# Rounding plain weight blocks by transfers: casting and adding DMAs in place of an ACT cast and a DVE subtract

## The chip, the cores and the metric

The kernel runs on one core of a Trainium2 chip. The metric is the device time of one execution in microseconds (us), lower is better. The core has five engines with their own instruction streams: TensorE (PE, matmuls; PEld are its weight loads), VectorE (DVE), ScalarE (ACT), GpSimd (POOL) and SyncE (SP), beside 16 DMA engines that the streams of SP, ACT and POOL can feed. The engines meet through semaphores only; each runs its own stream in order.

## The reference

One inference step of a decoder layer on 560 token columns: 16 meta tokens, 512 prompt tokens, 32 new tokens of 8 running sequences. With D = 1024 and a feed-forward width of 2816 = 22 x 128:

```python
x = x + 0.5 * swiglu(rmsnorm(x, g1), w_gate1, w_up1, w_down1)     # FFN1
x = x + mixer(rmsnorm(x, gm), ...)                                # mLSTM heads and RG-LRU
x = x + 0.5 * swiglu(rmsnorm(x, g2), w_gate2, w_up2, w_down2)     # FFN2
y = rmsnorm(x, gf)
```

where `swiglu(x, g, u, d) = (silu(x @ g) * (x @ u)) @ d`. Everything is fp32. The change touches the two FFNs only.

## The kernel before

**Three products for one.** PE multiplies in fp32r, a rounded fp32. To keep fp32's precision each operand is split into a rounded part `hi` and its remainder `lo`, and a product becomes three: hi by hi, hi by lo, lo by hi (`split_mm`, the matmuls are L295). Weights come from HBM in units of 128 x 512 (the down projections' in part 128 x 384). Of each unit the first product reads `whi`, the second `whi` again, the third `wlo`, for each of its 128-column pieces, so PE needs `wlo` about 0.5 us behind the unit's first matmul.

**The weight pipeline.** `units` lists all weight units in the order of use, each with a kind. Kind `""` is a plain block. The kinds "11", "s2", "s1" and so on belong to the seven-product form, in which the later blocks of both FFNs are multiplied from sums of quarters. For a plain unit there are three steps before: `load` puts an SP transfer into a `raw` tile, `split_hi` rounds it on ACT (a cast, L258) into `whi`, `split_lo` subtracts on DVE (L263) into `wlo`. Each fetch of a unit (`next_w`) first calls `run_ahead`, which emits the load of the unit 8 ahead, sums 6 ahead, the cast 5 ahead and the subtract 4 ahead (`AHEAD = 8, 6, 5, 4`). `raw`, `whi` and `wlo` have six buffers each, so a unit's tile is free when the unit six before it has been multiplied.

**Plain blocks at the beginnings.** A block is 128 of the 2816 hidden columns: a gate product g, an up product u (two units each) and a part of the down products d0 to d7. FFN1 has the first 4 blocks plain (`PLAIN = 4, 3`), FFN2 the first 3. FFN1 starts with pieces of block 0, loaded by code of its own; then come g1, u1, g2, u2, g3, u3 and the down units d4, d0, d2, d6, d5, d3, d1, d7. FFN2 has g0, u0, g1, u1, g2, u2 and eight down units of 384 columns. Everything behind is in the seven-product form.

**What sets the order.** PE, ACT and DVE are in `MANUAL`: their instructions stay in the order in which the program emits them, and that order is written out in the lists `FF1`, `FF2`, `MID1` and `MID2` as step names. POOL and SP are ordered by a scheduler. Of the steps, `g2` or `u1` are products, `eg`/`eu` scale them into `z`, `sg` is the Silu on ACT (L538), `mu`, `hh` and `hl` make the hidden tile and its two parts (L534, L544, L547); `ya`/`yb` form the normalised input `xn` for the seven-product form (DVE, L553), `Ah`, `Bh`, `Eh` and `Fh` round pieces of it on ACT (L560, tiles q11h, q21h, qt1h, qt4h), `ta` to `td` make its differences on DVE (L574 to L586). These steps are spread between the plain products. The piece of FF1 that matters here:

```python
... hh0 Ah1 u1 sg1 Bh1 hl0 Al1 eu1 g2 mu1 u2 ta1 Bl1 tb1 hh1 eg2 eu2 ...
```

A product step emits the ACT and DVE work of `run_ahead` at its own place in their streams, so a cast or subtract stands among the steps that are listed there. POOL does little in the FFNs: it adds up squares for the norms (`acc`, L377).

Of the kernel before, what the change touches and what calls it, by code (L numbers as in the profile page):

```python
# [5 lines left out]
F32 = mybir.dt.float32  # L6
F32R = mybir.dt.float32r
AF = mybir.ActivationFunctionType
ALU = mybir.AluOpType
PSUM = bass.MemoryType.PSUM  # L10

P = 128
# [4 lines left out]
TQ = T - C16  # L17
NP = 528
Q = 280
AHEAD = 8, 6, 5, 4  # L20
MANUAL = {mybir.EngineType.PE, mybir.EngineType.Activation, mybir.EngineType.DVE}
TCUT = 304
DED = 7
# [115 lines left out]
def hymba_step(ctx, tc, xT, wgu1, wdn1, win, wout, wgu2, wdn2, consts, small, c0t, wrg,  # L139
               y, o_small, o_m, o_cp, o_cs):  # L140
    nc = tc.nc
    act, dve, pool, pe = nc.scalar, nc.vector, nc.gpsimd, nc.tensor
# [10 lines left out]

    units = []

    def plain_units(w, n=1024):
        units.extend(("", w[:, c:min(c + 512, n)]) for c in range(0, n, 512))

    def units7(quarters):
        old = None  # L160
        for q in quarters:
            units.append(("11", q))
            if old is not None:
                units.extend((k, old) for k in ("22", "s4"))
            units.extend((k, q) for k in (("s2", "s1", "s3", "12") if old is not None else ("12", "s2", "s1", "s3")))
            old = q
        units.extend((k, old) for k in ("22", "s4"))

    def down_units(wdn, d, a, b):
        for i in range(a, b, 4):  # L170
            plain_units(wdn[d, :, i * P:min(i + 4, b) * P], (min(i + 4, b) - i) * P)

    def blocks(ff):


        a, b = PLAIN[ff], PLAIN[ff] + 8
        return (0, a), (a, b), {"d": (b, KF), "e": (b, FT), "t": (FT, KF)}

    def ff_units(ff, wgu, wdn, plan, mid):
        plain, seven, rest = blocks(ff)  # L180
        for t in plan:
            if t[0] in "gu" and t[1:].isdigit() or t[:2] == "ga":
                plain_units(wgu[int(t.lstrip("gua")), "gu".index(t[0])])
            elif t[0] == "d" and t[1:].isdigit():
                down_units(wdn, int(t[1:]), *plain)
        units7({"11": w[0, :, :512], "12": w[0, :, 512:], "21": w[1, :, :512], "22": w[1, :, 512:]}
               for w in (wgu[f] for f in range(seven[0], KF)))
        q = {}
        for t in mid:
            what, d = t[:-1], t[-1]  # L190
            if what in rest:
                down_units(wdn, int(d), *rest[what])
            elif what == "qa":
                lo, hi = (slice(i * P, i * P + 512) for i in (seven[0], seven[0] + 4))
                u, v = wdn[int(d)], wdn[int(d) + 4]
                q[d] = {"11": u[:, lo], "12": u[:, hi], "21": v[:, lo], "22": v[:, hi]}
            if what[:1] == "q":
                units.append((SEVEN[what[1]][0], q[d]))
    ff_units(0, wgu1, wdn1, FF1, MID1)
    for i in range(25):  # L200
        plain_units(win[i])
    for d in range(KD):
        plain_units(wout[d])
    ff_units(1, wgu2, wdn2, FF2, MID2)
    for d in range(TAIL, KD):
        down_units(wdn2, d, FT, KF)
    loaded, ready = {}, {}
    state = {"use": 0}

    def raw_tile():  # L210
        return wp.tile([P, 512], F32, tag="raw", name="raw")

    def hl_tile():
        return (wp.tile([P, 512], F32R, tag="hi", name="whi"), wp.tile([P, 512], F32R, tag="lo", name="wlo"))
# [6 lines left out]
    def load(i):  # L221
        kind, src = units[i]
        if not kind:
            loaded[i] = raw_tile()
            nc.sync.dma_start(loaded[i][:, :src.shape[-1]], src)
        for k in {"11": ("11",), "s2": ("21", "22"), "12": ("12",)}.get(kind, ()):
            t = raw_tile()
            nc.sync.dma_start(t, src[k])
            src[k] = t

    def quarter_sum(q, k):

        if k in q:
            return
        q[k] = q["s2"] if k == "s4" else sp.tile([P, 512], F32, tag="s", name=k, bufs=4)
        x, y, op = {"s1": ("21", "22", ALU.add), "s2": ("s1", "11", ALU.subtract),
                    "s3": ("11", "21", ALU.subtract), "s4": ("12", "s2", ALU.subtract)}[k]
        dve.tensor_tensor(q[k], q[x], q[y], op=op)  # L238

    def sums(i):  # L240
        kind, q = units[i]
        for k in {"s2": ("s1", "s2"), "s3": ("s3",)}.get(kind, ()):
            quarter_sum(q, k)
        b = units[i - 1 - AHEAD[1] + AHEAD[3]]
        if b[0] == "s2":
# [5 lines left out]
    def source(i):  # L251
        kind, q = units[i]
        return q[kind] if kind else loaded[i][:, :q.shape[-1]]

    def split_hi(i):
        ready[i] = hl_tile()
        src = source(i)
        act.copy(ready[i][0][:, :src.shape[-1]], src)  # L258

    def split_lo(i):  # L260
        src = source(i)
        hi, lo = (t[:, :src.shape[-1]] for t in ready[i])
        dve.tensor_tensor(lo, src, hi, op=ALU.subtract)  # L263

    def run_ahead(i):
        for fn, n in zip((load, sums, split_hi, split_lo), AHEAD):
            for j in range(state.get(fn, 0), min(i + n, len(units) - 1) + 1):
                fn(j)
                state[fn] = j + 1

    def up_to(i):
        for fn, n in ((load, 4), (sums, 0), (split_hi, 0), (split_lo, 0)):
            for j in range(state.get(fn, 0), i + n + 1):
                fn(j)
                state[fn] = j + 1

    def next_w(ahead=True):
        i = state["use"]
        state["use"] += 1
        if ahead:  # L280
            run_ahead(i)
        return ready.pop(i)
# [65 lines left out]
    class Norm:  # L348
# [38 lines left out]
        def mean(self):  # L387
            self.ps = [aux_tile("psn")[:, :(T - self.c0) // 2] for _ in range(2)]
            for hf in range(2):
                pe.matmul(self.ps[hf], one_m[1024], self.acc[:, self.half(hf)], start=True, stop=True)  # L390
            self.t = tmp("rn")
# [114 lines left out]
    def ffn(ff, nrm, c0, hp, plan, mid, steps):  # L506
# [87 lines left out]
        def rd(what):  # L594
            def fn(d):
                resid(ps[what, d], d, c0)
            return fn

        steps.update(ga=first_half, gb=second_half, g=product("g"), u=product("u"), pn=nrm.mean, rs=nrm.table, nw=nrm.step, eg=scaled("g"), eu=scaled("u"), sg=sg, mu=mu,
                     hh=hh, hl=hl, ya=y(0), yb=y(1), ta=ta, tb=tb, tc=tc_, td=td, d=dn("d", *plain), rd=rd("d"), v=run_ahead)  # L600
        for name, i, names, w in (("A", 0, ("11",), n), ("B", 1, ("21", "22"), 2 * n), ("E", 0, ("t1", "t3"), 2 * n),
                                  ("F", 1, ("t4", "t2"), 2 * n)):
# [117 lines left out]
    with tc.tile_pool(name="hp2", bufs=1) as hp, tc.tile_pool(name="sp2", bufs=1) as sp:  # L720
# [26 lines left out]
        w = [[next_w() for i in range(2)] for d in range(TAIL, KD)]  # L747
# [33 lines left out]
        with tc.manual_schedule(engines=MANUAL):  # L781
# [3 lines left out]
            a, b = parts[0]  # L785
            last_mm(1, TAIL, fs[:4])
            ps, t = mean(0)
# [11 lines left out]
            a, b = parts[1]  # L799
            ps, t = mean(1)  # L800
# [791 lines left out]
```

## Time and profile before

| | us |
|---|---|
| median of 3 runs | 1029.77 (1029.45 to 1031.06) |
| the profiled execution, its own time | 1030.47 |
| span of its profile | 1028.7 |
| mean granted clock of PE | 0.997 |

The profile is of one execution. Engine busy times are on its page; chains of waits name what released each step; a window's row gives busy time by engine, the granted TensorE clock and what the DMA engines moved. In a timeline row an entry such as `x3 1.89` is three instructions in a row that take 1.89 us together, and `[1.61 <-DVE xn L553]` is idle time ahead of it and what ended that. The plain blocks of FFN1 lie between 15 and 85 us, those of FFN2 between 651 and 708 us.

### The profile page before, as it was taken

To read this page: it belongs to the slowest core of one execution; us is meant where nothing else is said; L and a number is where in the kernel's file an instruction comes from. 1 tells how busy PE (TensorE), PEld (TensorE's weight loads), DVE (VectorE), ACT (ScalarE), POOL (GpSimd) and SP (SyncE) were. 2 spreads that over 40 slices of the span, in tenths; PEclk is the share of its full clock that TensorE was granted. 3 is DMA by queue.
4 is the path that set the end of the run, shared out by engine and by line. 5 is a ranking of instruction groups with operands and counts; after the bars stand their busy time and mean duration, and the time that the engine had idled before them with its cause. 6 is when DMAs were issued, how large, how long until landed. Compare 5 with 4: busy or idle time off the path is not lost.

```text
span 1028.7 us, 20136 instructions
## 1 busy us (share of the span) xinstructions
PE 1009.9 (98%) x7786; PEld 994.2 (97%) x7786; DVE 835.1 (81%) x1453; ACT 558.0 (54%) x1071; POOL 114.3 (11%) x178
## 2 busy tenths in 40 slices
PE   9999999999999999999999999999999999999996
PEld 8999999999999999989889999999999999999996
DVE  7988788888778797888878775789888889859774
ACT  6544555565544455575856643554555566653543
POOL 0000000000000043544442101100000000000003
PEclk9999999999999999999999999999999999999999
DMA  6322323233332334224132123123332323333222
GB/s 217 104 82 87 99 93 113 84 102 103 88 103 68 105 102 138 92 64 128 62 107 86 62 92 120 59 68 101 103 104 93 113 93 103 95 109 93 72 76 87
DMA packets 57543, 99.57 MB, mean 97 GB/s; under 512 B 7904, under 2 KB 14688, under 8 KB 57448
## 3 DMA queue, kind: packets, MB, share of 16 engines
q1 hardware_dynamic: 57304, 98.17, 30.3%
q8 instruction: 61, 1.00, 0.4%
q14 instruction: 34, 0.28, 0.1%
q10 hardware_dynamic: 144, 0.12, 0.0%
HBM read 93.57 MB, written 4.70 MB: 96 GB/s over the span
## 4 chain that ended last, share of the span: by engine, by line
PE 86%; DVE 6%; ACT 3%; issue 2%; POOL 1%; DMA 1%; SPq 0%; DVEq 0%; ACTq 0%; POOLq 0%
PE pb L408 27%; PE pad L408 20%; PE pd L295 14%; PE po L295 6%; PE pg L295 3%; PE pu L295 3%; PE py L295 2%; DVE wlo L263 1%; PE pv L295 1%; PE pk L295 1%; PE pq L295 1%; PE pd L762 1%; PE pn L1370 1%; PE p L295 1%; PE px L295 1%
## 5 line engine op out<-in xcount | busy, mean ns | idle before, releaser
L258 ACT CAST whi<-raw 128x512 fp32r<-128x512 f32 (+2 forms) x289 | 172.6, 606 | 164.6 <-PE pad L408 41.9
L263 DVE TENSOR_TENSOR wlo<-raw,whi 128x512 fp32r<-128x512 f32 (+2 forms) x289 | 197.1, 698 | 69.0 <-ACT whi L258 68.8
L258 ACT CAST whi<-s 128x512 fp32r<-128x512 f32 x180 | 111.8, 621 | 106.1 <-PE pb L408 36.5
L263 DVE TENSOR_TENSOR wlo<-s,whi 128x512 fp32r<-128x512 f32 x180 | 124.2, 691 | 12.7 <-ACT whi L258 6.5
L408 PE MATMUL pad<-q21h,whi 128*128 128x280 f32 (+1 forms) x360 | 104.2, 289 | 0.9 <-ACT whi L258 0.9
L408 PE MATMUL pb<-qt4l,whi 128*128 128x280 f32 (+1 forms) x360 | 104.0, 289 | 0.0
L408 PE MATMUL pad<-q21l,whi 128*128 128x280 f32 (+1 forms) x360 | 104.0, 289 | 0.0
L408 PE MATMUL pad<-q21h,wlo 128*128 128x280 f32 (+1 forms) x360 | 104.0, 289 | 0.0
L408 PE MATMUL pb<-qt4h,whi 128*128 128x280 f32 (+1 forms) x360 | 103.9, 289 | 0.0
L408 PE MATMUL pb<-qt4h,wlo 128*128 128x280 f32 (+1 forms) x360 | 103.9, 289 | 0.0
L408 PEld LDWEIGHTS pad<-q21h,whi 128*128 128x128 f32 x360 | 67.8, 188 | 1.1 <-ACT whi L258 1.1
L408 PEld LDWEIGHTS pb<-qt4h,whi 128*128 128x128 f32 x360 | 67.9, 189 | 0.0
L408 PEld LDWEIGHTS pb<-qt4h,wlo 128*128 128x128 f32 x360 | 67.8, 188 | 0.0
L408 PEld LDWEIGHTS pad<-q21l,whi 128*128 128x128 f32 x360 | 67.8, 188 | 0.0
L408 PEld LDWEIGHTS pb<-qt4l,whi 128*128 128x128 f32 x360 | 67.8, 188 | 0.0
L408 PEld LDWEIGHTS pad<-q21h,wlo 128*128 128x128 f32 x360 | 67.8, 188 | 0.0
L377 POOL TENSOR_TENSOR acc<-acc,sq 128x560 f32<-128x560 f32 (+1 forms) x12 | 18.1, 1512 | 442.9 <-ACT sq L376 442.7
L238 DVE TENSOR_TENSOR s<-raw 128x512 f32<-128x512 f32 x90 | 61.5, 683 | 2.1 <-DMA raw<-in_wdn 2.1
L295 PE MATMUL pd<-hl,whi 128*128 128x280 f32 (+1 forms) x294 | 61.6, 291 | 0.8 <-DVE hl L547 0.8
L295 PE MATMUL pd<-hh,whi 128*128 128x280 f32 (+1 forms) x294 | 61.3, 290 | 0.8 <-ACT hh L544 0.8
L295 PE MATMUL pd<-hh,wlo 128*128 128x280 f32 (+1 forms) x294 | 61.2, 289 | 0.0
L408 PE MATMUL pb<-q11h,whi 128*128 128x280 f32 (+1 forms) x180 | 52.4, 291 | 0.0
(456 smaller groups left out, 2978.6 us busy)
## 6 DMA issues: line engine op xcount, KB each, us to landing
raw<-in_wgu SPq DMA_DIRECT2D x174, 256.0 KB, 2.9
raw<-in_wdn SPq DMA_DIRECT2D x71, 256.0 KB, 2.8
raw<-in_win SPq DMA_DIRECT2D x50, 256.0 KB, 2.9
raw<-in_wout SPq DMA_DIRECT2D x16, 256.0 KB, 2.7
raw<-in_wdn SPq DMA_DIRECT2D x18, 192.0 KB, 2.4
c<-in_c0t SPq DMA_DIRECT2D x4, 512.0 KB, 3.5
out_o_cs<-c SPq DMA_DIRECT2D x4, 512.0 KB, 4.5
X<-in_xT SPq DMA_DIRECT2D x7, 280.0 KB, 4.3
```

Source lines behind the costliest of these rows:

```text
L238: dve.tensor_tensor(q[k], q[x], q[y], op=op)
L258: act.copy(ready[i][0][:, :src.shape[-1]], src)
L263: dve.tensor_tensor(lo, src, hi, op=ALU.subtract)
L295: state["mm"] = pe.matmul(ps[:, hf, :n], a[:, ws], b[k][:, c0 + hf * n:c0 + hf * n + n], start=first and j == 0 and i == 0, stop=last and ...
L377: (dve if d == KD - 1 else pool).tensor_tensor(self.acc[:, c0:], self.acc[:, c0:], s[:, c0:], op=ALU.add)
L408: pe.matmul(ps, a[:, k * P:k * P + P], b, start=first and k == 0 and i == 0, stop=k == KD // 2 - 1 and i == 2, skip_group_check=not first)
L762: pe.matmul(pd[d - TAIL][:, hf, :b - a], u[:, o:o + P], v[:, C16 + a:C16 + b], start=f == c0 and m == 0, stop=f == c1 - 1 and m == 2)
L1370: pe.matmul(pn[:, 0, a:512], V[:KROWS[i], i, :P], W[:KROWS[i], WO[i]:WO[i] + 512 - a], start=i == 0, stop=i == 4)
```

## The change

Units of plain blocks behind the first four of the program get the kind "dma": g2, u2, g3, u3 and the eight down units of FFN1 (16 units), and all plain units of FFN2 (20). For these,

- `load` puts out no SP transfer, and no `raw` tile is used;
- `split_hi` is a transfer from HBM on POOL's queue whose destination is fp32r, so that the transfer rounds (L264);
- `split_lo` does nothing;
- a fifth stage, `rest`, 3 units ahead, writes the negative of `whi` into `wlo` on ACT (L273), and a second transfer on POOL's queue adds the same weights from HBM to it (L274): `wlo = -whi + w`.

Per unit this is one SP transfer, one ACT cast and one DVE subtract less, and one ACT negative and two POOL transfers more. Lines behind the change move by 18 (the matmuls of L295 are L313, q11h's cast of L560 is L578).

```diff
-AHEAD = 8, 6, 5, 4
+AHEAD = 8, 6, 5, 4, 3
...
         for t in plan:
+            kind = "dma" if ff or len(units) > 3 else ""
...
-                plain_units(wgu[int(t.lstrip("gua")), "gu".index(t[0])])
+                plain_units(wgu[int(t.lstrip("gua")), "gu".index(t[0])], kind=kind)
...
-                down_units(wdn, int(t[1:]), *plain)
+                down_units(wdn, int(t[1:]), *plain, kind)
...
     def load(i):
...
+        if kind == "dma":
+            return
...
     def split_hi(i):
         ready[i] = hl_tile()
+        kind, src = units[i]
+        if kind == "dma":
+            pool.dma_start(ready[i][0][:, :src.shape[-1]], src)
+            return
         src = source(i)
         act.copy(ready[i][0][:, :src.shape[-1]], src)
 
+    def rest(i):
+        kind, src = units[i]
+        if kind == "dma":
+            hi, lo = (t[:, :src.shape[-1]] for t in ready[i])
+            act.mul(lo, hi.bitcast(F32), -1.0)
+            pool.dma_start(lo, src, accum_op=ALU.add)
+
     def split_lo(i):
+        if units[i][0] == "dma":
+            return
...
     def run_ahead(i):
-        for fn, n in zip((load, sums, split_hi, split_lo), AHEAD):
+        for fn, n in zip((load, sums, split_hi, split_lo, rest), AHEAD):
```

ACT's stream in FFN1, from the cast of u1's second half on (whi_403 before, whi_391 now). Before, 406 and 409 are the two halves of g2, 412 and 468 those of u2, 498 the first of g3:

```order
L258 CAST whi_403<-raw_315 128x512
L258 CAST whi_406<-raw_317 128x512
L258 CAST whi_409<-raw_328 128x512
L258 CAST whi_412<-raw_376 128x512
L560 CAST qt1h0_444<-xn_383 128x560
L560 CAST qt4h0_452<-xn_385 128x560
L544 CAST hh0_129<-z_394 128x560
L560 CAST q11h1_462<-xn_457 128x280
L258 CAST whi_468<-raw_397 128x512
L258 CAST whi_498<-raw_399 128x512
```

The same stretch now, where 394/395 and 397/398 are the rounded part and rest of g2's halves, and 400/401 of u2's first:

```order
L267 CAST whi_391<-raw_315 128x512
L273 ACTIVATE wlo_395<-whi_394 128x512
L578 CAST qt1h0_432<-xn_377 128x560
L578 CAST qt4h0_440<-xn_379 128x560
L562 CAST hh0_129<-z_388 128x560
L578 CAST q11h1_450<-xn_445 128x280
L273 ACTIVATE wlo_398<-whi_397 128x512
L273 ACTIVATE wlo_401<-whi_400 128x512
L556 ACTIVATE z_438<-z_438 128x560
```

Both halves of g2 were rounded on ACT ahead of qt1h0; now the negative of the second half stands behind q11h1, and its adding transfer behind that.

POOL's stream in FFN1 behind the constants, now (before, nothing stood there up to FFN1's end; 483 and 521 are g3's halves, 455 the second of u2):

```order
L264 DMA whi_483<-in_wgu1 128x512
L274 DMA wlo_395<-in_wgu1 128x512
L264 DMA whi_521<-in_wgu1 128x512
L274 DMA wlo_398<-in_wgu1 128x512
L274 DMA wlo_401<-in_wgu1 128x512
L274 DMA wlo_455<-in_wgu1 128x512
L274 DMA wlo_484<-in_wgu1 128x512
```

Casting transfers, which wait for a free buffer, and adding ones, which wait for ACT's negative, alternate in one queue at first.

ACT's stream in FFN2's down units, before:

```order
L560 CAST qt4h2_8791<-xn_8767 128x544
L258 CAST whi_8797<-raw_8664 128x384
L560 CAST q11h3_8822<-xn_8819 128x272
```

and now, where 8668 is the rest of the fourth down unit and 8697 of the fifth:

```order
L578 CAST qt4h2_8749<-xn_8725 128x544
L273 ACTIVATE wlo_8668<-whi_8667 128x384
L578 CAST q11h3_8781<-xn_8778 128x272
L273 ACTIVATE wlo_8697<-whi_8696 128x384
L273 ACTIVATE wlo_8756<-whi_8755 128x384
```

The cast that stood there was of a later unit (the sixth); now it is the fourth unit's negative, with a transfer still to come.

POOL's stream at the beginning of FFN2, now; before, the three acc rows stood there without a transfer between them:

```order
L264 DMA whi_8124<-in_wgu2 128x512
L274 DMA wlo_8096<-in_wgu2 128x512
L395 TENSOR_TENSOR acc_5034<-acc_5034,sq_8185 128x544
L264 DMA whi_8151<-in_wgu2 128x512
L274 DMA wlo_8125<-in_wgu2 128x512
L264 DMA whi_8189<-in_wgu2 128x512
L274 DMA wlo_8152<-in_wgu2 128x512
L395 TENSOR_TENSOR acc_5034<-acc_5034,sq_8252 128x544
```

The accumulations of FFN2's norm now stand behind the transfers of its first units.

More of the change, by code (lines that the diff above doesn't have):

```diff
@@ L154, in hymba_step, with plain_units @@
     units = []
-    def plain_units(w, n=1024):
-        units.extend(("", w[:, c:min(c + 512, n)]) for c in range(0, n, 512))
+    def plain_units(w, n=1024, kind=""):
+        units.extend((kind, w[:, c:min(c + 512, n)]) for c in range(0, n, 512))
     def units7(quarters):
@@ L167, in units7, with down_units @@
         units.extend((k, old) for k in ("22", "s4"))
-    def down_units(wdn, d, a, b):
+    def down_units(wdn, d, a, b, kind=""):
         for i in range(a, b, 4):
-            plain_units(wdn[d, :, i * P:min(i + 4, b) * P], (min(i + 4, b) - i) * P)
+            plain_units(wdn[d, :, i * P:min(i + 4, b) * P], (min(i + 4, b) - i) * P, kind)
     def blocks(ff):
```

## The prediction

> **What bounds the kernel now.** I read the page first: the busy line, then the chain of waits by engine, then the transfer rates of the first slices.
>
> ```profile
> span 1028.7 us, 20136 instructions
> PE 1009.9 (98%) x7786; PEld 994.2 (97%) x7786; DVE 835.1 (81%) x1453; ACT 558.0 (54%) x1071; POOL 114.3 (11%) x178
> GB/s 217 104 82 87 99 93 113 84 102 103 88 103 68 105 102 138 92 64 128 62 107 86 62 92 120 59 68 101 103 104 93 113 93 103 95 109 93 72 76 87
> PE 86%; DVE 6%; ACT 3%; issue 2%; POOL 1%; DMA 1%; SPq 0%; DVEq 0%; ACTq 0%; POOLq 0%
> ```
>
> TensorE is busy for 98% of the span and holds 86% of the chain. So work taken from DVE or ACT buys nothing in itself; it counts where PE waits. How much waiting there is, the windows over the plain blocks show: three over FFN1's (15 to 85 us), two over FFN2's (651 to 708 us). Columns are the window, its length, the busy time (instructions) of PE, PEld, DVE, ACT and POOL, the granted clock, the DMA share and GB/s.
>
> ```profile
> 15.00:35.00 20.00, 19.04 (x139) 18.18 (x138) 17.31 (x31) 10.57 (x18) 0.00 (x0) 1.00 0.33 108
> 35.00:62.00 27.00, 27.00 (x210) 26.83 (x208) 22.45 (x37) 12.94 (x24) 0.00 (x0) 1.00 0.34 108
> 62.00:85.00 23.00, 22.75 (x175) 22.47 (x175) 21.96 (x38) 8.67 (x16) 0.00 (x0) 1.00 0.24 81
> 651.00:690.00 39.00, 38.70 (x306) 38.32 (x304) 32.34 (x58) 20.58 (x38) 1.67 (x2) 1.00 0.21 65
> 690.00:708.00 18.00, 16.99 (x132) 16.77 (x133) 17.93 (x33) 7.66 (x14) 0.00 (x0) 1.00 0.31 102
> ```
>
> PE's idle time there is 0.96 + 0 + 0.25 + 0.30 + 1.01 = 2.5 us. That is all that this change could win, and all that now covers it is lead time: how long before PE reads a weight half the half is ready.
>
> **What falls away.** 36 units (16 in FFN1, 20 in FFN2; 28 of 512 columns, 8 of 384) lose their SP load, ACT cast and DVE subtract.
>
> ```profile
> L258 ACT CAST whi<-raw 128x512 fp32r<-128x512 f32 (+2 forms) x289 | 172.6, 606 | 164.6 <-PE pad L408 41.9
> L263 DVE TENSOR_TENSOR wlo<-raw,whi 128x512 fp32r<-128x512 f32 (+2 forms) x289 | 197.1, 698 | 69.0 <-ACT whi L258 68.8
> L377 POOL TENSOR_TENSOR acc<-acc,sq 128x560 f32<-128x560 f32 (+1 forms) x12 | 18.1, 1512 | 442.9 <-ACT sq L376 442.7
> raw<-in_wgu SPq DMA_DIRECT2D x174, 256.0 KB, 2.9
> raw<-in_wdn SPq DMA_DIRECT2D x18, 192.0 KB, 2.4
> c<-in_c0t SPq DMA_DIRECT2D x4, 512.0 KB, 3.5
> Eb<-rows SPq DMA_DIRECT2D x4, 272.0 KB, 4.7
> ```
>
> DVE loses about 36 x 0.698 = 25 us of busy time (a little less for the 384-wide), all beside PE: 0 us on the path. ACT exchanges a cast of 0.606 for a negative of the same shape, one for one: 0 on the path as long as ACT stays near half busy (10.57 of 20.00 in the first window). The weights are read twice, 28 x 256 KB + 8 x 192 KB = 9 MB more; FFN1's 4.2 MB over 70 us are 60 GB/s beside 81 to 108, and the page's first slice moved 217, so bandwidth costs 0. If that cover were gone, it would lengthen each landing, which the upper bound below holds.
>
> **What is added: a longer tail behind each rounded half.** Before, the second half of a weight block was one DVE instruction of 0.698 us behind the cast. Now it is a negative on ACT, an issue on POOL's queue, and a transfer from HBM that adds into the tile. I call T the time from the start of that issue to the landing, and I the time of one POOL issue. The trace has neither a POOL transfer nor an adding one. T's lower bound is the fastest SP row of this size, 2.4 us (192 KB); the upper is the slowest, 4.7 (272 KB), and 0.6 for a slower issue: 5.3. I is bounded by SP's issue below (0.43) and a POOL TENSOR_TENSOR above (1.512).
>
> ```profile
> 5.06 0.43 SPq L633 DMA_DIRECT2D raw<-in_wgu  x1
> ```
>
> I take I = 1.0, the middle. I take T = 3.8: a transfer that also reads its destination moves between once and twice its bytes, so 2.9 (256 KB) to 3.5 (512 KB), and I - 0.43 = 0.6 more to issue gives 3.5 to 4.1. One page has a price: the Trainium skill, "DMA: Bandwidth & Descriptors", section "Anatomy of one DMA — SWDGE (gpsimd) path", fits 2.0 us + bytes/436e3 per transfer from this queue, an estimate of 2.6 us for 256 KB and a sum lower by 1.2; no run here shows it yet.
>
> **FFN1: the place that sets the end.** The new stage is emitted only 3 units ahead, and ACT's order puts the negative of g2's second half (wlo_398) behind q11h1, a step of Ah1 that waits for DVE's xn. The timeline of before at that place:
>
> ```profile
> 31.31 1.89 DVE L263 TENSOR_TENSOR wlo<-raw,whi 128x512 fp32r<-128x512 f32 x3
> ...
> 37.87 1.51 DVE L553 SCALAR_TENSOR_TENSOR xn<-X,C,r 128x560 f32<-128x560 f32 x2
> ...
> 38.37 0.42 PE L295 MATMUL pg<-xh,wlo 128*128 128x280 f32 x2
> ...
> 38.70 0.43 ACT L560 CAST q11h<-xn 128x280 fp32r<-128x280 f32 x1 [1.61 <-DVE xn L553]
> ...
> 39.03 0.62 ACT L258 CAST whi<-raw 128x512 fp32r<-128x512 f32 x1
> ```
>
> PE first reads that half at 38.37. Of the three subtracts at 31.31, two (g2's) are gone: 2 x 0.63 = 1.26 us. If DVE is earlier by all of it, q11h1 starts at 38.70 - 1.26 = 37.44 and ends at 37.87; the negative, 0.62 like the cast at 39.03, ends at 38.49; with 0.07 for a signal (38.70 less the first xn's end, 37.87 + 0.755) POOL issues at 38.56. The half lands at 38.56 + T, so PE is late by T + 0.2 = **4.0 us** (2.6 and 5.5 at T's bounds). If DVE's waits, 2.7 us in the first window, eat the 1.26, it is T + 1.45. On POOL only the casting transfer of g3 stands between; it waits for a buffer that u1's last matmul frees at 34.90 (chain row below) and is issued by 36. The earlier half of g2 may stall PE too; that moves PE's clock of needs, not the landing at 42.4, so the two don't add. The units behind follow one issue (1.0) apart while PE takes 6.21 / 2 = 3.1 us for each: covered. Queued on ACT behind the negative are u2's negative and g1's Silu; neither waits for POOL.
>
> ```profile
> 34.90 6.21 PE pg L295 x48
> ...
> 574.88 7.55 PE py L295 x48
> ...
> 588.96 6.03 PE py L295 x48
> ...
> 651.15 6.01 PE pg L295 x48
> ...
> 691.52 16.68 PE pd L295 x130
> ```
>
> **FFN2.** The tightest place is the fourth down unit (wlo_8668), whose negative stands behind qt4h2:
>
> ```profile
> 692.49 0.65 ACT L560 CAST qt4h<-xn 128x544 fp32r<-128x544 f32 x1 [2.09 <-DVE xn L586]
> 693.04 0.51 ACT L258 CAST whi<-raw 128x384 fp32r<-128x384 f32 x1
> ...
> 697.18 0.42 PE L295 MATMUL pd<-hh,wlo 128*128 128x272 f32 x2
> ```
>
> Negative to 693.04 + 0.51 = 693.55, issue at 693.6, landing at 693.6 + T against a need at 697.18: late by T - 3.6 = **0.2 us** (0 and 1.7 at the bounds).
>
> **The clock.** Chains show one unit pair on PE taking 7.55 us where the same work later took 6.03. The windows around the first, and around the 1.0 us of idle at 690:
>
> ```profile
> 569.00:574.00 5.00, 5.00 (x29) 3.54 (x28) 3.16 (x7) 4.34 (x8) 1.59 (x1) 1.00 0.02 3
> 574.00:578.00 4.00, 4.00 (x20) 3.96 (x21) 2.89 (x5) 2.97 (x7) 0.32 (x1) 0.57 0.00 0
> 690.00:693.00 3.00, 1.99 (x13) 1.77 (x14) 2.97 (x7) 0.91 (x2) 0.00 (x0) 1.00 0.00 0
> ```
>
> After 5 us of thin matmul work the granted clock fell to 0.57 and cost 7.55 - 6.03 = 1.5 us; after 1.0 us of idle it stayed at 1.00. A stall of 4 us with nothing at all is nearer the first: **+1.5 us**, between 0 and 1.5. The Trainium skill, "TensorE: Matmul & The Clock Gate", section "What's actually happening", says that a free-running window of about 3.4 us without activity halves the clock; a 4.0 us stall need not hold a whole window, so by that rule the term could be 0. The trace's fall after thin, not empty, work speaks for more.
>
> **Sum.** Against the profiled execution: 1030.47 + 4.0 + 0.2 + 1.5 = 1036.2 us. That execution lies 0.7 above the median of the runs, so the median comes to **1035.5 us**, +0.56%. Bounds: 1029.77 + 2.6 = 1032.4 (T = 2.4, no clock) to 1029.77 + 6.75 + 1.7 + 1.5 = 1039.7.
>
> **Rivals.**
>
> *B, POOL becomes the bound.* FFN2 has 40 issues. The first can't go before a hi buffer is free, five units of 6.01 / 2 = 3.0 us ahead of 651.15: 636.1. The last down unit starts about 2.3 us before the chain's end at 708.2 and reads its second half 0.5 later; less T, its issue must start by 702.6. In those 66.5 us POOL also does three accumulations for the norm:
>
> ```profile
> 653.26 1.37 POOL L377 TENSOR_TENSOR acc<-acc,sq 128x544 f32<-128x544 f32 x1 [1.96 <-ACT sq L376]
> ```
>
> (66.5 - 4.1) / 39 = 1.60 us for each issue: from I = 1.6 POOL decides. At I = 1.75 FFN2 pays 39 x 0.15 = 5.9, FFN1 T = 4.55 and so 4.75, the clock 1.5: 1029.77 + 12.1 = 1041.9. For it: in-order waits on negatives cost POOL some of that time, and those accumulations, which gate FFN2's norm, now queue behind transfers. Against: 1.6 is above the 1.51 of a whole elementwise pass on this engine. The Trainium skill, "SBUF — State Buffer", section "A bandwidth-pool intuition that's wrong (but worth ruling out)", has such a transfer grow from 620 to 3100 ns beside a DVE copy that shuts POOL out; its section "Who interferes with whom" infers that two-input subtracts, the rows here, leave descriptor writing alone. By the first, an issue that waits for one DVE instruction of 0.698 is an estimate of I = 1.7, in B.
>
> *C, hidden.* T below 1.9 us, or a DVE so much earlier that the negative no longer stands behind q11h1's wait: within 2.06 us of before, about 1029.8. Against: no SP row of 192 KB or more lands under 2.4, and DVE would have to gain 4 us there, not 1.26.
>
> *D, faster.* DVE's waits for casts and the late hh/hl at 690 to 693 close because 36 subtracts are gone, and PE's 2.5 us of idle with them: 1029.77 - 2.5 = 1027.3. It decides only if the negative of g2 is issued by 38.37 - 3.8 = 34.6, where DVE's gain would have to be 5.2 us instead of 1.26.
>
> **How the numbers follow.** The forecast (late landings) 0.68, B 0.17, C 0.09, D 0.06. About 0.2% (2.06 us) is what a measurement of this kernel can tell from no change; the forecast and B lie wholly above it: slower 0.85, same 0.09, faster 0.06. The forecast's own range is 1032.4 to 1039.7; B spreads from 1038 to 1050, so up to 1043 about two thirds of it are inside, and the lower end at 1031.8 leaves out C and D: 0.68 + 0.11, about 0.8, in 1031.8 to 1043.0.
>
> **What would show it.** Right: POOL transfers of some 3.8 us to landing; PE's largest new wait in g2 behind 38 us, ended by the DMA of wlo, 3 to 4 us long, with the granted clock below 1.00 in the windows after it; little at the fourth down unit of FFN2. B: POOL issues above 1.6 us back to back through 636 to 703, and PE's waits in FFN2 as large as in FFN1. Wrong: no DMA among what ended PE's waits in 35 to 45 us; or DVE's xn at 35 us rather than 36.6.

## The result, and the profile after

The changed kernel takes 1037.92 us (median of 5 runs, 1036.68 to 1039.34) against 1029.77 (5 runs) before: 8.15 us slower, ratio 1.0077 with a 95% interval of 1.0065 to 1.0089. The forecast was 1035.5 in 1031.8 to 1043.0, slower: the direction and the main place were right, the size was 5.7 us where 8.15 were measured.

The page of the kernel after, its span, busy times and chain by engine:

```profile
span 1036.2 us, 20166 instructions
PE 1012.5 (98%) x7786; PEld 996.2 (96%) x7786; DVE 813.7 (79%) x1417; ACT 557.0 (54%) x1071; POOL 166.7 (16%) x250
PE 77%; issue 5%; DVE 5%; POOL 5%; DMA 4%; ACT 3%; SPq 0%; DVEq 0%; POOLq 0%; ACTq 0%
```

DVE is busy 21.4 us less, ACT the same, and POOL and the transfers now hold 9% of the chain where they held 2%. The DMA issues of POOL's queue, with the median time from issue to landing:

```profile
whi<-in_wgu POOLq DMA_DIRECT2D x20, 256.0 KB, 4.7
wlo<-in_wgu POOLq DMA_DIRECT2D x20, 256.0 KB, 5.5
whi<-in_wdn POOLq DMA_DIRECT2D x8, 256.0 KB, 5.9
wlo<-in_wdn POOLq DMA_DIRECT2D x8, 256.0 KB, 4.4
whi<-in_wdn POOLq DMA_DIRECT2D x8, 192.0 KB, 3.9
wlo<-in_wdn POOLq DMA_DIRECT2D x8, 192.0 KB, 4.4
```

How long an issue holds POOL is in the rows of its two lines (duration min/median/max in ns), the casting one first:

```profile
L264 POOL DMA_DIRECT2D whi<-in_wgu x20: 527/556/1599, 19.7 to 674.7; - x20
...
L274 POOL DMA_DIRECT2D wlo<-in_wgu x20: 863/896/1602, 32.4 to 683.0; - x20
```

The timeline of the kernel after at g2 shows the waits:

```profile
32.38 0.90 POOL L274 DMA_DIRECT2D wlo<-in_wgu  x1 [0.20 <-issue]
...
38.05 0.53 PE L313 MATMUL pg<-xh,wlo 128*128 128x280 f32 x2 [2.07 <-DMA wlo<-in_wgu]
38.06 0.43 ACT L578 CAST q11h<-xn 128x280 fp32r<-128x280 f32 x1 [1.61 <-DVE xn L571]
38.39 1.15 ACT L273 ACTIVATE wlo<-whi 128x512 fp32r<-128x512 f32 x2
39.32 1.78 POOL L274 DMA_DIRECT2D wlo<-in_wgu  x2 [3.27 <-ACT wlo L273]
...
43.54 0.53 PE L313 MATMUL pg<-xh,wlo 128*128 128x280 f32 x2 [0.60 <-DMA wlo<-in_wgu]
```

and its windows there, with the granted clock behind the five busy times:

```profile
36.00:39.00 3.00, 0.95 (x7) 0.95 (x8) 3.00 (x5) 1.39 (x4) 0.05 (x1) 1.00 0.58 132
39.00:42.60 3.60, 3.60 (x19) 3.60 (x17) 3.50 (x7) 3.22 (x7) 2.90 (x5) 0.54 0.43 69
42.60:46.00 3.40, 2.79 (x21) 2.55 (x21) 0.02 (x1) 0.00 (x0) 2.08 (x3) 0.98 1.02 155
```

PE reads g2's second `wlo` at 43.54 where it read it at 38.37. The second place is the first down unit of FFN1, where a negative that waits for its casting transfer stands ahead of the hidden tile's cast on ACT; the third is FFN2's fourth down unit:

```profile
66.32 0.63 ACT L273 ACTIVATE wlo<-whi 128x512 fp32r<-128x512 f32 x1 [2.77 <-DMA whi<-in_wdn]
...
67.18 0.65 ACT L562 CAST hh<-z 128x560 fp32r<-128x560 f32 x1
...
67.88 0.53 PE L313 MATMUL pd<-hh,whi 128*128 128x280 f32 x2 [0.54 <-ACT hh L562]
...
697.65 0.52 ACT L273 ACTIVATE wlo<-whi 128x384 fp32r<-128x384 f32 x1
...
698.46 0.89 POOL L274 DMA_DIRECT2D wlo<-in_wdn  x1 [0.98 <-ACT wlo L273]
...
702.29 0.52 PE L313 MATMUL pd<-hh,wlo 128*128 128x272 f32 x2 [0.39 <-DMA wlo<-in_wdn]
```

The last place is the end of the program. The rows are its closing instructions (minimum, median and maximum in ns, first and last start); before:

```profile
L1573 POOLq DRAIN  x3: 34/78/1441, 1022.6 to 1028.4; - x3
L1573 SPq DRAIN  x3: 7/7/7, 1027.9 to 1028.2; - x3
```

and after:

```profile
L1591 POOLq DRAIN  x3: 40/102/7344, 1028.1 to 1035.9; - x3
L1591 SPq DRAIN  x3: 7/7/7, 1033.5 to 1035.7; - x3
```

POOL's first closing drain took 1.44 us before and was over when SP reached its own at 1027.9. Now it takes 7.34 us, from 1028.1 to 1035.4, while SP is at its drain at 1033.5: the program ends about 2 us later for it.

PE runs the same 7786 matmuls in the same order in both profiles, so the lag of each instruction behind its counterpart can be followed. It is 0.56 us just before the first changed unit is reached (nothing is changed up to there), 5.17 at g2's second half, 5.82 behind FFN1's first down unit, 4.53 behind the mixer, 5.48 at the last matmul and 7.53 at the end. So: start 0.56, g2 4.61, first down unit 0.65 (0.54 of it is the wait for `hh`), mixer -1.29, FFN2 0.95, end 2.05. The start and the mixer are not the change's. No kernel below changes anything there; they lie within 0 to 0.8 at the start, and gain 1.0 to 2.4 us on that one profile of before over the mixer. The profile of before has a stretch of 3.4 us at half clock in the mixer, at 574 us (quoted with the prediction), where no wait covered it. Seven other profiles have one somewhere in the mixer too. Five have none there (the two kernels with earlier negatives, casting alone, adding alone and the 72 small transfers), and in the first four of these the clock falls behind waits in the FFNs.

### The profile page after: what moved, and what is told of

Read it like the earlier page. It is cut to its first block, busy times and chain, and to the rows that moved or that the text cites. A ratio compares the mean times of both kernels' runs of the same rounds, so it can differ in the third digit from the quotient of the medians.

```text
span 1036.2 us, 20166 instructions
## 1 busy us (share of the span) xinstructions
PE 1012.5 (98%) x7786; PEld 996.2 (96%) x7786; DVE 813.7 (79%) x1417; ACT 557.0 (54%) x1071; POOL 166.7 (16%) x250
## 4 chain that ended last, share of the span: by engine, by line
PE 77%; issue 5%; DVE 5%; POOL 5%; DMA 4%; ACT 3%; SPq 0%; DVEq 0%; POOLq 0%; ACTq 0%
PE pb L426 26%; PE pad L426 20%; PE pd L313 14%; PE po L313 5%; PE py L313 2%; PE pv L313 2%; DMA whi<-in_wgu 1%; POOL wlo L274 1%; DVE wlo L281 1%; PE pq L313 1%; DMA whi<-in_wdn 1%; POOL whi L264 1%; PE pd L780 1%; PE pn L1388 1%; PE p L313 1%
## 5 line engine op out<-in xcount | busy, mean ns | idle before, releaser
L267 ACT CAST whi<-raw 128x512 fp32r<-128x512 f32 (+2 forms) x253 | 151.9, 608 | 144.3 <-PE pad L426 42.2
L281 DVE TENSOR_TENSOR wlo<-raw,whi 128x512 fp32r<-128x512 f32 (+2 forms) x253 | 174.9, 706 | 61.0 <-ACT whi L267 60.8
L313 PE MATMUL pd<-hh,whi 128*128 128x280 f32 (+1 forms) x294 | 61.4, 290 | 1.3 <-ACT hh L562 1.3
L313 PE MATMUL pd<-hl,whi 128*128 128x280 f32 (+1 forms) x294 | 61.5, 290 | 0.8 <-DVE hl L565 0.8
L313 PE MATMUL pd<-hh,wlo 128*128 128x280 f32 (+1 forms) x294 | 61.4, 290 | 0.4 <-DMA wlo<-in_wdn 0.4
L749 POOL TENSOR_TENSOR acc<-acc,sq 128x272 f32<-128x272 f32 (+2 forms) x10 | 10.0, 1018 | 297.8 <-ACT sq L747 297.8
```

What stands on the lines that cost most here:

```text
L313: state["mm"] = pe.matmul(ps[:, hf, :n], a[:, ws], b[k][:, c0 + hf * n:c0 + hf * n + n], start=first and j == 0 and i == 0, stop=last and ...
L749: pool.tensor_tensor(acc[:, a:b], acc[:, a:b], s, op=ALU.add)
```

## The experiments

Ratios are to runs of the kernel before on the same chip (medians 1029.12, 1028.76 and 1029.00 us for the three groups).

**One transfer pair in FFN2.** The units that the change marks are set back to plain except one:

```diff
+    first2 = max(i for i in range(1, len(units)) if units[i][0] == "dma" and units[i - 1][0] != "dma")
+    for i, (kind, src) in enumerate(units):
+        if kind == "dma" and i not in (first2,):
+            units[i] = "", src
```

> Only the first unit of FFN2 takes the casting and the adding transfer; all others stay as before, and this unit has slack (in the profile of the change PE waited for nothing there). Theory (a fixed price at the end: once POOL has issued a transfer, its last drain took 7.35 us instead of 1.44): the last matmul ends as before, the POOL drain is some 6 us longer than its last instruction, and the kernel is slower by about 1.9 us, 1031.7. Rival (the end's 2 us come from the 72 transfers or are chance): 1029.8, within 0.5 us of before.

1029.48 us, ratio 1.0003 (0.9995 to 1.0012): no change, the rival holds. The closing drain was hardly longer than before:

```profile
L1595 POOLq DRAIN  x3: 40/93/1629, 1021.1 to 1026.8; - x3
```

So the price at the end is no fixed one. It grows with something.

**FFN2 alone, FFN1 alone.**

```diff
-            kind = "dma" if ff or len(units) > 3 else ""
+            kind = "dma" if ff else ""                            # FFN2 alone
+            kind = "dma" if not ff and len(units) > 3 else ""     # FFN1 alone
```

> The 20 plain units of FFN2 changed, FFN1 as before. Theory of late landings (0.6 us at the fourth and 0.3 at the fifth or sixth down unit) and the end's 1.9: slower by 2.8, 1032.6. Rival B (POOL the bound in FFN2): more than 5 us slower, 1034.8 or above, with POOL issues without gaps between 636 and 703 us.

> The 16 units of FFN1 changed, FFN2 as before. Theory: 4.6 us at g2, 0.65 at the first down unit, 1.9 at the end, less up to 1.3 that the mixer gave back in the profile of the change: slower by 5.9 to 7.2, 1035.7 to 1037.0. If most of the loss were FFN2's or the end's: under 1033.

FFN2 alone: 1030.93, ratio 1.0016 (1.0007 to 1.0025), 1.8 us slower. FFN1 alone: 1035.11, ratio 1.0057 (1.0043 to 1.0071), 6.0 slower. Over FFN2 the lag grows by 2.0 us in the profile of FFN2 alone, where the change had 0.95; a wait of 0.59 for an up unit's half and 1.1 at the down units are in it, so these landings vary from one execution to the next. Most of the loss is FFN1's, and rival B of the prediction (POOL the bound of FFN2) falls. The closing drains say more. FFN1 alone, with 32 transfers:

```profile
L1591 POOLq DRAIN  x3: 40/102/4077, 1026.6 to 1032.8; - x3
L1591 SPq DRAIN  x3: 7/7/7, 1032.3 to 1032.6; - x3
```

FFN2 alone, with 40:

```profile
L1591 POOLq DRAIN  x3: 40/102/4732, 1023.3 to 1029.2; - x3
L1591 SPq DRAIN  x3: 7/7/7, 1028.7 to 1029.0; - x3
```

Both end ahead of SP's. From 32 to 72 transfers the drain grows by (7.34 - 4.08) / 40 = 0.082 us for each.

**g2 and u2 plain.**

```diff
-            kind = "dma" if ff or len(units) > 3 else ""
+            kind = "dma" if ff or len(units) > 7 else ""
```

> As the change, but g2's and u2's four units stay plain, so no negative stands behind q11h1 with a unit right behind it. Theory (the order at g2 is what costs in FFN1): g2's 4.6 us are gone, what is left is 0.65 (first down unit), 0.9 (FFN2) and 1.9 (end): slower than before by 3.5, 1033.3. Rival (the landing is late at whatever unit comes first): the same stall of 4 to 5 us at g3, 1037 to 1038.

1031.98, ratio 1.0025 (1.0015 to 1.0034). FFN1's stall is gone and did not move to g3. Windows over FFN1 of this kernel:

```profile
35.00:62.00 27.00, 27.00 (x211) 27.00 (x211) 17.75 (x30) 11.49 (x21) 11.28 (x16) 1.00 0.83 182
62.00:85.00 23.00, 22.69 (x175) 22.23 (x174) 20.03 (x35) 10.09 (x18) 5.49 (x7) 1.00 0.67 133
```

PE is busy throughout as before, with 12 units of FFN1 changed; the lag stays at 0.3 us from 24 to 98 us, so here the change neither costs nor brings anything, although DVE has 4.7 us less to do in the first of these windows. It is 1.3 us better than expected: the 0.65 at the first down unit went too. What is left in its profile is 1.7 us of lag that grows in FFN2 and an end that is 1.4 us longer with 64 transfers (9.40 us from the last matmul instead of 8.01).

**The negative and the adding transfer earlier: 5 ahead.**

```diff
-AHEAD = 8, 6, 5, 4, 3
+AHEAD = 8, 6, 5, 4, 5
```

> AHEAD 5 instead of 3 for the stage with the negative and the adding transfer: both negatives of g2 now stand ahead of q11h1 on ACT. POOL still has g3's casting transfer, which waits for a buffer, ahead of g2's first adding one. Theory (the order on ACT makes the second half of g2 late, the queue on POOL the first): the wait of 2.0 us at g2's first half stays, the one at its second half goes, and the half clock that follows the first wait is no longer covered: with it 2.0 + 1.7, without it 2.0. So 0.9 us faster than the change with a fall of the clock (1037.0), 2.6 faster without (1035.3). Rival (landing time alone, whatever the order): as the change, 1037.9.

1052.93, ratio 1.0233 (1.0219 to 1.0248): 24 us slower than before, and neither theory had that. At g2 the reading was right (one wait of 2.7 us, then a clock fall, no wait at the second half, 4.4 us of lag in all), but the rest of the program paid. The timeline of this kernel at FFN2's norm:

```profile
661.77 0.63 ACT L273 ACTIVATE wlo<-whi 128x512 fp32r<-128x512 f32 x1 [4.24 <-DMA whi<-in_wgu]
662.30 0.73 ACT L383 ACTIVATE xh<-X,C 128x544 fp32r<-128x544 f32 x1
```

and its waits of PE:

```profile
PE pd L313 <- ACT hh L562: 5.3, 2, 3.2
PE pg L313 <- ACT xh L383: 3.1, 3, 1.7
PE pg L313 <- DMA wlo<-in_wgu: 2.7, 1, 2.7
```

A negative that is emitted together with its casting transfer stands on ACT until that has landed, and what is behind it on ACT (here `xh`, elsewhere `hh`) is late for PE. Falls of the clock behind these waits are part of the loss: the granted clock was 0.50 from 70 to 73 us, 0.52 from 667 to 674 and 0.57 from 708 to 712.

**4 ahead.**

```diff
-AHEAD = 8, 6, 5, 4, 3
+AHEAD = 8, 6, 5, 4, 4
```

> The change with AHEAD 4 instead of 3 for the negative and the adding transfer: as with 5 ahead, g2's second negative now stands ahead of q11h1, but one unit later than the casting transfer's issue, not together with it. Theory (a negative that is placed early holds ACT until its casting transfer lands, and the steps behind it, xh of FFN2's norm above all, are late): between 3 and 5 ahead, 1040 to 1046, with waits of PE for ACT's xh in FFN2. Rival (the order at q11h1 alone matters): 1 us faster than the change, 1037.

1044.79, ratio 1.0147 (1.0130 to 1.0163): between 3 and 5 ahead, as the blocking theory has it. PE's waits here are 4.4 us for ACT's `hh`, 0.9 for `xh` and 2.8 for one late landing; the theory had named `xh` above all. The granted clock was 0.50 from 69.4 to 76.2 us, from within the longer wait for `hh` on. Put late, the adding transfer lands late; put early, the negative holds ACT for the casting transfer: with this lead there was no good place among the three tried.

**The casting transfer alone, the adding transfer alone.** In the first the rest is DVE's subtract from an SP load as before; in the second the rounded half is ACT's cast of an SP load as before.

```diff
     def load(i):
-        if not kind:
+        if kind in ("", "dma"):
...
     def rest(i):                      # the casting transfer alone
-        if kind == "dma":
-            hi, lo = (t[:, :src.shape[-1]] for t in ready[i])
-            act.mul(lo, hi.bitcast(F32), -1.0)
-            pool.dma_start(lo, src, accum_op=ALU.add)
+        return
     def split_lo(i):
-        if units[i][0] == "dma":
-            return
...
     def split_hi(i):                  # the adding transfer alone
-        if kind == "dma":
-            pool.dma_start(ready[i][0][:, :src.shape[-1]], src)
-            return
```

> The rounded half by the casting transfer on POOL, the rest by SP's load and DVE's subtract as before; no negative and no adding transfer. Theory (the tail behind the rounded half costs, the casting transfers have lead enough): no wait at g2, only the end's 1.9: 1031.7. Rival (POOL transfers as such cost, by bandwidth or a late rounding): 1034 or above.

> The rounded half by SP's load and ACT's cast as before, the rest by the negative and the adding transfer. Theory: the wait at g2's second half stays whole (its negative still stands behind q11h1), a wait at its first half is 0.5 us shorter for want of a casting transfer ahead of it; at the first down unit of FFN1 no negative waits for a casting transfer, so 0.65 us less; the end's 1.9 stays: 4.6 + 0.9 + 1.9 less up to 1.3, slower than before by 6 to 7.4, 1035.8 to 1037.2. Rival (the casting transfers make the loss): 1032.

Casting alone: 1032.10, ratio 1.0030 (1.0020 to 1.0040). The number is near the expected one, the reason is not: with 36 transfers the drain (4.40 us) ends ahead of SP's. FFN1 has no wait for a weight, as expected. The profiled execution is the slowest of the ten (1034.73 us); its loss lies at FFN2's norm, around 656 us:

```profile
652.17 0.69 DVE L276 TENSOR_TENSOR wlo<-raw,whi 128x512 fp32r<-128x512 f32 x1 [1.69 <-issue]
652.53 1.55 POOL L390 TENSOR_TENSOR acc<-acc,sq 128x544 f32<-128x544 f32 x1 [0.91 <-ACT sq L389]
652.78 1.88 DVE L379 SCALAR_TENSOR_TENSOR xl<-X,C,xh 128x544 fp32r<-128x544 f32 x1
...
656.13 0.52 PE L308 MATMUL pg<-xh,whi 128*128 128x272 f32 x2 [0.65 <-ACT xh L378]
656.95 0.52 PE L308 MATMUL pg<-xl,whi 128*128 128x272 f32 x2 [0.30 <-DVE xl L379]
```

The casting transfer issued at 646.94 landed after 5.15 us, the longest of the 36 (median 3.2), and DVE's subtract starts 0.08 us behind that landing. `xl` stands behind the subtract on DVE and took 1.88 us over a POOL accumulation, where its neighbours take 0.79. The next `xh` and PE were late by it, and the clock fell as well (0.57 from 658 to 662 us). That the late landing began this is read from one execution and was not tried apart; what costs the median execution its 3.3 us stays open.

Adding alone: 1042.46, ratio 1.0129 (1.0114 to 1.0143), 13.7 us slower than before where the whole change is 8.15 slower, and above its expectation. PE's waits in its timeline:

```profile
39.59 0.56 PE L310 MATMUL pg<-xh,wlo 128*128 128x280 f32 x2 [3.93 <-DMA wlo<-in_wgu]
45.15 0.52 PE L310 MATMUL pg<-xh,wlo 128*128 128x280 f32 x2 [0.67 <-DMA wlo<-in_wgu]
...
707.69 0.52 PE L310 MATMUL pd<-hh,wlo 128*128 128x272 f32 x2 [2.82 <-DMA wlo<-in_wdn]
```

The places are those of the change, the waits longer. The first negative of g2 now stands behind four casts on ACT, its transfer is issued at 33.64 instead of 32.38, and lands after 5.9 us; the fourth down unit's is issued at 701.80 and lands after 5.8 us, where the change had 3.8. Behind that wait the granted clock was 0.50 from 709.0 to 712.4 us. So without casting transfers the loss is larger than the change's, and without adding ones it is 3.3 us with none in FFN1: most of the loss comes with the adding transfers. Why this one landed 2 us slower is open.

**One unit of g2 alone: its second half, then its first.** As the first experiment, with one other unit kept:

```diff
+        if kind == "dma" and i not in (5,):      # second half of g2;  (4,): first half
+            units[i] = "", src
```

> Only the second half of g2 in FFN1, one unit of the whole program, takes the two transfers. Theory: PE waits once, 4.5 to 5.2 us in one piece; the clock then halves for 3.4 us and costs 1.7, which no later landing covers; and the end's 1.9: slower by 8.1 to 8.8, 1037.9 to 1038.6, as slow as the whole change. Without a fall of the clock 1036.2 to 1036.9. Rival (the loss is spread over the 36 units): 1032.

> Only the first half of g2 takes the two transfers. Its negative stands ahead of qt1h0 and no casting transfer ahead of it on POOL: issue at 32.1, landing 4.2 to 5.6 us later, a wait of 1.0 to 2.4 us. Theory: the clock halves behind it as behind the 2.1 us in the change, and now no later landing covers it: 1.0 to 2.4 + 1.7 = 2.7 to 4.1 slower, 1031.8 to 1033.2. Rival (it is the wait for the second half that pulls the clock down): 1.0 to 2.4 slower.

The second half alone: 1037.86, ratio 1.0083 (1.0070 to 1.0096). One unit of 36 makes the kernel as slow as the whole change, though not by the change's terms: g2 costs 4.6 us there and 8.5 here. Its windows:

```profile
38.00:45.00 7.00, 0.47 (x4) 0.25 (x2) 6.08 (x11) 4.14 (x8) 0.89 (x1) 0.77 0.63 156
45.00:49.00 4.00, 3.75 (x17) 3.75 (x18) 0.00 (x0) 0.00 (x0) 0.00 (x0) 0.54 0.35 121
49.00:52.00 3.00, 3.00 (x25) 3.00 (x25) 1.90 (x4) 0.62 (x1) 0.00 (x0) 1.00 0.07 11
```

PE waits 6.8 us in one piece, and then runs 17 matmuls in a window that holds some 33 at full clock: the lag grows from 6.88 to 8.52. That is the price of a clock fall with nothing to cover it, 1.6 us. The expected total came true by luck, with other terms: a longer wait (the issue is at 39.87, the landing 5.3 us later), and no price at the end with 2 transfers.

The first half alone: 1033.58, ratio 1.0037 (1.0024 to 1.0050), 4.6 us slower. In its profiled execution (1031.64 us) PE waited 2.81 us for the landing (issued at 33.46, 5.3 us) and the clock stayed at 1.00 through the windows behind:

```profile
36.00:38.00 2.00, 0.00 (x1) 0.00 (x0) 1.93 (x4) 1.07 (x2) 0.00 (x0) 1.00 0.65 109
38.00:40.00 2.00, 1.19 (x9) 1.19 (x10) 2.00 (x4) 1.32 (x3) 0.00 (x0) 1.00 0.01 2
40.00:42.00 2.00, 2.00 (x17) 2.00 (x17) 2.00 (x4) 2.00 (x5) 0.00 (x0) 1.00 0.36 104
```

The five runs are 1031.64, 1032.24, 1033.58, 1033.96 and 1034.27; the median is 1.9 above the profiled one, about what a fall costs, so in some executions the fall may have followed this wait. The profile can't show that, since it is of an execution without it, and the mean granted clocks of the five runs (0.993 to 0.997) do not follow their times.

**72 small transfers, no unit changed.** The kernel before, with

```diff
+    spare = cst.tile([P, 32], F32, name="spare")
+    def extra(i):
+        if 60 <= i < 132:
+            j = i % 4 * 8
+            pool.dma_start(spare[:, j:j + 8], wgu1[0, 0][:, :8])
     def run_ahead(i):
-        for fn, n in zip((load, sums, split_hi, split_lo), AHEAD):
+        for fn, n in zip((load, sums, split_hi, split_lo, extra), AHEAD + (0,)):
```

> The kernel before, with 72 small transfers (128 x 8, 4 KB) added on POOL's queue into a tile that nothing reads; no weight unit changed, and every result computed as before. Theory (the last drain of POOL grows by 0.082 us for each transfer that POOL has issued, as the drains of 1.6 us after 2 transfers, 4.07 after 32, 6.69 after 64 and 7.35 after 72 suggest, and passes SP's end from about 48 on): POOL's last drain takes 7.35 us, the time from the last matmul to the end is 10.0 instead of 8.0, and the kernel is 2.0 us slower, 1031.0. Rival (the drain depends on bytes, or is that of adding transfers alone): no change, 1029.0.

1031.27, ratio 1.0020 (1.0011 to 1.0029), 2.3 us slower. All 72 are issued in the first 60 us, hundreds of us before the end, and the closing rows are:

```profile
L1580 POOLq DRAIN  x3: 40/102/7346, 1021.1 to 1029.0; - x3
L1580 SPq DRAIN  x3: 7/7/7, 1026.9 to 1028.7; - x3
```

The drain is that of the change to within 2 ns, with 4 KB instead of 256 KB to a transfer and no adding one. From the last matmul to the end it takes 10.06 us, as after the change, where it took 8.01 before. The packets of POOL's queue differ too, 32 to a small transfer and 144 to one of the change, and 36 casting transfers alone and 36 adding ones alone both give 4.40 us. So the number of transfers sets it, not their bytes, packets or kind, and this part of the loss is shown.

No version that beats the kernel before came out: with 12 units of FFN1 changed at no cost, PE gained nothing either: from 35 to 85 us it idled 0.25 us before and 0.31 in that kernel, with fewer subtracts.

## Why the prediction was right or wrong

**What bounds the kernel: right.** The 21.4 us less on DVE (25 taken) and the casts' removal bought nothing in any run.

**FFN1, g2's second half: right place, right queue, 4.0 against 4.6.** The profile after runs 0.56 us late before anything is changed, so its times are read less that. DVE then gained what was taken: q11h1 starts at 38.06 - 0.56 = 37.50 (37.44 taken). From the negative's end to the issue it took 0.3 us (39.02 to 39.32), where 0.07 was read from DVE to ACT; the same 0.29 to 0.31 stands behind a negative at 21 issues of the change, while an accumulation on POOL starts 0.08 to 0.15 us behind ACT's square. The half landed 4.18 us after its issue (3.8 taken). So the issue was 0.2 us later than taken and the landing took 0.4 longer, the 0.6 between 4.0 and 4.6. That the first half's stall would not add to it held too: PE waited 2.07 there and only 0.60 at the second. The single wait of 3 to 4 us that was named as the sign did not come, since the first half's wait and the half clock took its place.

**The clock, +1.5: right that it falls, wrong that it adds.** It fell to half for 3.4 us behind the first wait, inside the time in which PE had to wait for the second half anyway. Half clock or idle, PE resumed at the landing. The step that failed is the sum, which took the stall as one piece of 4 us with the fall behind it. Where it is one piece (g2's second half alone) the fall costs 1.6. The Trainium skill, "TensorE: Matmul & The Clock Gate", section "What's actually happening", gives a binary gate and a free-running window of about 3.4 us. The traces agree: the clock is 0.50 for 3.413 us or twice that, and in the change the stretches of full clock ahead of its two falls before the closing are 34.13 and 498.35 us, 10 and 146 times 3.413. On that grid the wait of 2.07 us lies within one step (35.88 to 39.29 us), and the fall follows; the wait of 2.81 us (g2's first half alone), which no fall followed, is split over two steps, 1.47 and 1.34 us. The step ahead of a fall need not be wholly idle: PE was busy for 1.34 of its 3.41 us in the change.

**FFN2's fourth down unit: right place, 0.2 against 0.95 over FFN2.** Issue to landing was 3.8 us, as taken; the issue stood 0.3 us behind the negative's end, so this unit cost 0.6, and a further 0.28 came at the unit behind it.

**"Queued on ACT behind the negative ... neither waits for POOL": wrong.** At that place nothing waited (the two negatives from 38.39 on ran without a gap). Elsewhere negatives on ACT wait for casting transfers, and what stands behind them waits too: up to 0.65 us at the first down unit. With the negatives 4 and 5 ahead the kernels lose 15.8 and 24.2 us instead of 8.15, with waits of PE for `hh` and `xh` and falls of the clock behind them. The prediction priced the wait on POOL's side only.

**The end of the program: missed, 2.05.** It is the largest term that the sum lacked. With g2 at 4.6, the first down unit at 0.65, FFN2 at 0.95 and the end at 2.05 the change costs 8.26, against 8.15 measured. So the forecast came as near as it did partly by luck: the 1.5 for the clock, which did not come, stood in for most of the 2.05 at the end, which was not foreseen.

**Rival B: wrong.** An issue takes 0.56 us (casting) or 0.90 (adding) in the median, and 1.6 only at the longest, where 1.0 was taken and 1.6 was the limit; POOL was busy for 24.07 of the 49 us from 651 to 700. The two prices of the Trainium skill weighed there come out on the side of its "SBUF — State Buffer", section "Who interferes with whom": beside the two-input subtract of `hl` the adding issue of g2's second half alone took 0.89 us, and the three adding issues of the change with nothing on DVE beside them took 0.89 to 0.93. C and D fell with the landings and with PE's unchanged waits.

## What to carry to other kernels

A transfer in place of a short instruction lengthens the lead that a value needs by its issue and landing (here 3.6 to 8.0 us instead of 0.7), so price it at the place with the least lead, with the in-order queue ahead of it on every engine that touches it; the two halves of g2, 2 of 36 units, made 4.6 of the 8.15 us here. A wait that is moved onto an engine's queue must be paid on both sides: late negatives made PE wait for weights, early ones made it wait for what stood behind them. And look at the program's end: work on a queue can leave a bill there long after its last use.

## What the hardware showed that was not expected

- POOL's closing drain grows by 0.082 us for each transfer that POOL issued anywhere in the program: 1.44 us with none, 1.63 after 2, 4.08 after 32, 4.73 after 40, 6.69 after 64, 7.34 after 72. In this program it sets the end once it outlasts SP's closing waits. Before, these ended at 1027.9, 3.9 us behind the drain's end (1022.6 + 1.4), so an estimate is 3.9 / 0.082, about 48 transfers; with 40 the drain was over ahead of SP's waits, with 64 the end came 1.4 us later.
- An adding transfer of 256 KB landed 4.2 to 5.3 us after its issue with no other adding one in the program; in the change the adding ones took 3.6 to 8.0, the casting ones 2.7 to 7.8. Issues that come back to back were up to 1.6 us long. What sets a landing within these ranges stays open.
- A clock fall costs nothing where PE would have waited through it (3.4 us at half clock in the change), and 1.6 us where PE had work (g2's second half alone). Falls keep to a grid of 3.413 us, so the length of a wait alone does not tell whether one follows: 2.07 us brought one in the change, 2.81 us in the profile of g2's first half alone none.
